# Element operations of two SBUF inputs moved from GpSimd to VectorE, squares and the convolution's first term to ScalarE, in a two-layer encoder trunk

## The chip, the core and the metric

The kernel runs on one core of one Trainium2 chip. The metric is the device time of one execution in microseconds (us), the median over runs. VectorE is called DVE here, ScalarE ACT, GpSimd POOL, the matrix engine (TensorE) PE and its weight loads PEld, SyncE SP, as in the profile. Every engine works through its own queue strictly in order, and waits at the head of the queue until what the next instruction needs is there.

## What is computed

A trunk of two layers over 1024 frames of width 1024, all in float32. The reference, cut to what matters:

```python
c_act = silu(c)
mod = c_act @ ada_w[layer] + ada_b[layer]          # six vectors of shift, scale and gate
hn = modulate(rms_norm(h, norm1_g[layer]), sh1, sc1)
# layer 0: z = hn @ w_in; gate, xr = split(z); xr = causal_depthwise_conv(xr, conv_w, conv_b)
#   r, i = sigmoid(block products of xr); a = exp(-8 r softplus(-lam)); scan a*h + mult*(i*xr)
#   y = (scan * gelu(gate)) @ w_out
# layer 1: y = chunked attention of own queries against keys and values shared from layer 0
h = h + g1 * y
hn = modulate(rms_norm(h, norm2_g[layer]), sh2, sc2)
h = h + g2 * (square(relu(hn @ w1)) @ w2)
```

The result has to agree with this in float32, so each product is made of three fast ones: every operand is split into a rounded high part and the rest, its low part, and `mm3` adds high*high, high*low and low*high.

## The kernel before

Frames lie along the free axis in two halves of 512, features along the 128 partitions. ACT makes each high part with a copy, and another engine the low part with a subtraction. Seven stretches follow each other:

- To about 100 us: norm of x, modulation, the first three products (`sq_b`, `normed`, `moded`, `lows`).
- To about 420 us, called the recurrent stretch here: for each of 11 column tiles a gate and a recurrent product, the width-4 convolution (`conv`, L700: a first term on DVE at L703, three further taps at L706), the split of its result (L283), and for each of 16 blocks of 88 features the gates and the scan (`lru`, L728: sums and products on DVE at L756 to L761, the product i*x on POOL at L759). Weight low parts are made at L192, here by POOL, since `ws.lo_engine` starts as POOL. Between these DVE makes the modulation vectors by multiplying rows of `ada` with c (L310). POOL also multiplies the scan's result by the gate (`flush`, L724) and splits it (`split_yg`, L772).
- To about 545 us: the output projection, with the residual added by DVE (L584); then to 617 us the second norm, the plain first quarter of the MLP, and the sums and splits of its operands (`NormS.mod`, `NormS.sums`, `part`).
- 617 to 917 us, the first MLP product of layer 0: 14 steps (`Quads.step`), each of seven products of 12 matmuls, in the manner of Strassen. A step needs sums of weight blocks (`add_quad`, four instructions at L124, on POOL), the splits of weights and of their sums (ACT L188, low parts L192 on DVE), the reads of the seven results (ACT L1104 for the first three, DVE L1106 for three that add, ACT L1109 for the last), relu and square (DVE L1042 and L1110), and sums of hidden blocks that are then stored to memory (`store`, four instructions at L1032, on POOL). Up to three L310 are put between.
- 917 to 1250 us, the second MLP product: 15 steps of the same form; the hidden blocks are loaded back and split (L192 on DVE, twelve of the first ones on POOL through `eng=G`), and all seven results are added by DVE (L1127).
- 1250 to 1860 us: queries, keys, values, attention and its projection.
- 1866 to 2536 us: the MLP of layer 1, with no L310 in it; its first product takes 1930 to 2207 us.

What sets the order: outside the MLPs a scheduler does. Within them the order is written out by hand: a tick passes after each of the seven products; weight sums are issued no sooner than two ticks behind the issue of their loads (`LAG`), low parts wait in the list `ws.los` and are let out by `Stream.flush`, those for DVE up to three half tiles a tick and those for POOL at once; `store` puts its jobs 1, 3 and 7 ticks later. A step's results use three PSUM banks; a bank that a second product adds to is free again once the first has been read, and two products lie between.

## Time and profile before

| | |
|---|---|
| median of 3 runs | 2536.57 us (2536.54 to 2541.02) |
| profiled execution: its own time, and the span from first to last instruction | 2537.57 us, 2535.7 us |
| granted TensorE clock, mean over the span | 0.963 |
| PE, PEld busy | 2318.8 us, 1953.4 us |
| DVE, ACT, POOL busy | 1881.2 us, 1132.7 us, 1158.5 us |
| instructions of DVE, ACT, POOL | 2300, 1835, 792 |

Busy time is the time in which an engine has an instruction in work. Matmuls are pipelined, so a busy PE is not necessarily one at its full rate; the count of matmuls in a stretch of time tells that better. A group's row gives line, engine, operation, output and inputs, shape, the count, then the busy time and the mean of one in ns, and last the engine's idle time just ahead of these instructions with what ended it. Rows of stretches give for each engine its busy time and count, then the granted clock, the share of time that the DMA engines were busy, and GB/s.

### The profile page before, as it was taken

What the parts mean: (1) busy time and instruction counts of PE and PEld (TensorE: products, weight loads), DVE (VectorE), ACT (ScalarE), POOL (GpSimd) and SP (SyncE); (2) the same over time, 40 slices, a digit from 0 to 9 for tenths busy, and PEclk for the clock granted to TensorE, in tenths of its full rate; (3) what the DMA queues carried; (4) which work ended last, traced back from release to release, by engine and by line L of the source; (5) the groups of instructions that cost most, each with busy time, mean ns of one, the idle gap of its engine ahead of it and who ended that gap; (6) DMA issues with size and microseconds to landing.
All of it is one profiled execution on the core that took longest, in us unless ns stands there. A gap on an engine that the chain in (4) does not pass through costs nothing.

```text
span 2535.7 us, 31960 instructions
## 1 busy us (share of the span) xinstructions
PE 2318.8 (91%) x11740; PEld 1953.4 (77%) x11740; DVE 1881.2 (74%) x2300; ACT 1132.7 (45%) x1835; POOL 1158.5 (46%) x792
## 2 busy tenths in 40 slices
PE   4989876987999969999999999999998999889999
PEld 3767654866777857888899998998876888667887
DVE  8879887678888877778675466998377656767776
ACT  5577653344222333334354216998153332433342
POOL 3535434337676763332011026885047666642322
PEclk9989897998999989999999999999999999999999
DMA  7323455213565576545444300012313454765444
GB/s 289 116 79 82 111 158 177 66 71 129 194 229 214 198 244 200 153 150 170 152 132 132 117 5 11 10 28 87 126 38 121 163 182 158 238 230 159 139 151 142
DMA packets 138061, 351.93 MB, mean 139 GB/s; under 512 B 14160, under 2 KB 16336, under 8 KB 137904
## 3 DMA queue, kind: packets, MB, share of 16 engines
q1 hardware_dynamic: 114080, 278.45, 34.4%
q10 hardware_dynamic: 23824, 71.44, 7.4%
q8 instruction: 92, 1.51, 0.3%
q14 instruction: 65, 0.53, 0.1%
HBM read 254.42 MB, written 83.89 MB: 133 GB/s over the span
## 4 chain that ended last, share of the span: by engine, by line
PE 56%; DVE 19%; DMA 8%; ACT 8%; issue 5%; POOL 4%; SPq 1%; ACTq 0%; DVEq 0%; POOLq 0%
PE b L278 17%; PE b L279 17%; PE b L277 17%; DMA ws<-in_ada_dram 3%; DVE s L310 2%; POOL ws L124 2%; DMA ws<-in_w_dram 2%; DVE s L192 2%; DVE ws L310 2%; PE b L1467 1%; DVE wl L192 1%; ACT s L1437 1%; DVE s L706 1%; ACT s L282 1%; ACT wh L188 1%
## 5 line engine op out<-in xcount | busy, mean ns | idle before, releaser
L277 PE MATMUL b<-s,wh 128*128 128x512 f32 x2532 | 1006.4, 401 | 115.7 <-DVE s L1106 31.3
L278 PE MATMUL b<-s,wh 128*128 128x512 f32 x2532 | 1009.3, 399 | 50.4 <-DVE s L283 42.5
L279 PE MATMUL b<-s,wl 128*128 128x512 f32 (+1 forms) x2296 | 911.4, 397 | 5.3 <-POOL wl L192 4.0
L277 PEld LDWEIGHTS b<-s,wh 128*128 128x128 f32 x2532 | 484.8, 192 | 240.1 <-DVE s L1106 34.7
L278 PEld LDWEIGHTS b<-s,wh 128*128 128x128 f32 x2532 | 486.3, 192 | 164.9 <-DVE s L283 46.2
L188 ACT ACTIVATE wh<-ws 128x1024 fp32r<-128x1024 f32 (+1 forms) x302 | 293.1, 974 | 569.3 <-POOL ws L124 298.7
L279 PEld LDWEIGHTS b<-s,wl 128*128 128x128 f32 (+1 forms) x2296 | 438.6, 191 | 104.9 <-POOL wl L192 5.3
L192 DVE TENSOR_TENSOR wl<-ws,wh 128x1024 fp32r<-128x1024 f32 (+1 forms) x212 | 322.3, 1522 | 137.4 <-ACT wh L188 120.4
L124 POOL TENSOR_TENSOR ws<-ws,ws 128x512 f32<-128x512 f32 x145 | 237.1, 1635 | 69.0 <-DMA ws<-in_w_dram 61.5
L124 POOL TENSOR_TENSOR ws<-ws 128x512 f32<-128x512 f32 x53 | 74.6, 1407 | 407.8 <-DMA ws<-in_w_dram 315.1
L192 DVE TENSOR_TENSOR s<-ws,s 128x512 fp32r<-128x512 f32 x238 | 227.7, 964 | 2.6 <-ACT s L188 2.6
L1127 DVE SCALAR_TENSOR_TENSOR s<-b,mod,s 128x512 f32<-128x512 f32 x221 | 165.0, 746 | 81.0 <-PE b L279 81.0
L277 PE MATMUL b<-wh,s 128*128 128x256 f32 x768 | 217.5, 285 | 2.6 <-ACT s L501 1.6
L279 PE MATMUL b<-wh,s 128*128 128x256 f32 x768 | 215.1, 284 | 3.5 <-DVE s L502 2.4
L278 PE MATMUL b<-wl,s 128*128 128x256 f32 x768 | 217.0, 284 | 0.0
L1032 POOL TENSOR_TENSOR s<-s,s 128x512 f32<-128x512 f32 x96 | 166.1, 1731 | 49.4 <-DMA hid<-s 44.4
L188 ACT ACTIVATE s<-ws 128x512 fp32r<-128x512 f32 x262 | 151.8, 618 | 64.1 <-PE b L279 30.8
L310 DVE CUSTOM_DVE_ANT_0 ws<-ws,cb,vec 128x1024 f32<-128x1024 f32 x64 | 96.5, 1511 | 110.5 <-DMA ws<-in_ada_dram 110.5
L192 POOL TENSOR_TENSOR wl<-ws,wh 128x1024 fp32r<-128x1024 f32 (+2 forms) x37 | 96.5, 2614 | 150.8 <-ACT wh L188 150.7
L277 PEld LDWEIGHTS b<-wh,s 128*128 128x128 f32 x768 | 147.9, 193 | 3.2 <-ACT s L501 1.8
L279 PEld LDWEIGHTS b<-wh,s 128*128 128x128 f32 x768 | 146.6, 193 | 4.3 <-DVE s L502 3.0
L278 PEld LDWEIGHTS b<-wl,s 128*128 128x128 f32 x768 | 148.0, 193 | 0.3 <-issue 0.2
(182 smaller groups left out, 3396.4 us busy)
## 6 DMA issues: line engine op xcount, KB each, us to landing
hid<-s ACTq DMA_DIRECT2D x128, 512.0 KB
ws<-hid SPq DMA_DIRECT2D x118, 512.0 KB
ws<-in_w_dram SPq DMA_DIRECT2D x220, 256.0 KB
ws<-in_ada_dram SPq DMA_DIRECT2D x64, 512.0 KB
s<-in_ada_dram SPq DMA_DIRECT2D x32, 512.0 KB
ws<-in_w_in_dram SPq DMA_DIRECT2D x22, 512.0 KB
hsp<-s SPq DMA_DIRECT2D x32, 256.0 KB
s<-in_kvada_dram SPq DMA_DIRECT2D x16, 512.0 KB
```

The costliest lines, as they stand in the source:

```text
L124: G.tensor_tensor(out=out, in0=in0, in1=in1, op=op)
L188: self.nc.scalar.activation(out=hi[:rows, :n], in_=src, func=AF.Copy)
L192: (it["eng"] or self.lo_engine).tensor_tensor(out=lo[:rows, :n], in0=src, in1=hi[:rows, :n].bitcast(F32), op=ALU.subtract)
L277: PE.matmul(ps, ah, bh, start=start, stop=False, skip_group_check=more)
L278: PE.matmul(ps, ah, bl, start=False, stop=False, skip_group_check=more)
L279: return PE.matmul(ps, al, bh, start=False, stop=stop, skip_group_check=more).ins
L282: A_.activation(out=hi, in_=src, func=AF.Copy)
L310: V.tensor_tensor_reduce(out=t, in0=t, in1=cb, op0=ALU.mult, op1=ALU.add, scale=1.0, scalar=bias, accum_out=dst)
L706: V.scalar_tensor_tensor(out=y[:, d:], in0=xr[:, : S - d], scalar=vc("cw", (3 - d) * NT + t), in1=y[:, d:], op0=ALU.mult, op1=ALU.add)
L1032: G.tensor_tensor(out=out, in0=in0, in1=in1, op=ALU.subtract)
L1127: V.scalar_tensor_tensor(out=t, in0=ps, scalar=g2[:, m : m + 1], in1=t, op0=ALU.mult, op1=ALU.add)
L1437: A_.activation(out=p[:, lo:640], in_=p[:, lo:640], func=AF.Exp, scale=-1.0, bias=m, accum_out=s1)
```

## The change

420 instructions leave POOL. Its remaining work is the weight sums of the second MLP products from the third step on, and what attention gives it. DVE takes over all the others: 61 low parts of weights and hidden blocks (L192), 128 sums of hidden blocks (L1032), 128 of the 236 weight-sum instructions (L124), the low parts of norms and of the gated result (L499, L537, L772, L818), sums of the norms (L552, L801), and the products L724 and L759. DVE gives away the convolution's first term (L703), which ACT makes while it reads the result from PSUM, and all squares behind relu (L1042, L1055, L1110): `relu2` is now two ACT instructions, relu and square, and for the three results that DVE adds they are issued one tick later. ACT's `Identity` with a bias and a DVE instruction replace two ACT copies where POOL had made the low part (`modulate`). `Stream.flush` lets out four half tiles a tick, not three, and `store` puts its jobs 2, 4 and 8 ticks later. The diff, cut to its core:

```diff
-    def add_quad(self, a11, a12, a21, a22, n):
+    def add_quad(self, a11, a12, a21, a22, n, eng):
...
-                G.tensor_tensor(out=out, in0=in0, in1=in1, op=op)
+                eng.tensor_tensor(out=out, in0=in0, in1=in1, op=op)
...
             def low():
-                (it["eng"] or self.lo_engine).tensor_tensor(
+                self.nc.vector.tensor_tensor(
                     out=lo[:rows, :n], in0=src, in1=hi[:rows, :n].bitcast(F32), op=ALU.subtract)
...
-    def flush(self, most=3):
+    def flush(self, most=4):
...
-            ws.add_quad(u[:, :512], u[:, 512:], v[:, :512], v[:, 512:], 512)
+            ws.add_quad(u[:, :512], u[:, 512:], v[:, :512], v[:, 512:], 512, V)
...
-            ws.add_quad(*(I["w2"][l][s % 4][x][:, c] for x in range(4)), 512)
+            ws.add_quad(*(I["w2"][l][s % 4][x][:, c] for x in range(4)), 512, G if s > 1 else V)
...
-        if pool:
-            A_.activation(out=t, in_=t, func=AF.Identity, bias=sh[:, k : k + 1])
-            N.lastact = A_.activation(out=hi, in_=t, func=AF.Copy).ins
-            G.tensor_tensor(out=lo, in0=t, in1=hi.bitcast(F32), op=ALU.subtract)
-        else:
-            A_.activation(out=hi, in_=t, func=AF.Identity, bias=sh[:, k : k + 1])
-            V.scalar_tensor_tensor(out=lo, in0=t, scalar=sh[:, k : k + 1], in1=hi.bitcast(F32),
-                                   op0=ALU.add, op1=ALU.subtract)
+        A_.activation(out=hi, in_=t, func=AF.Identity, bias=sh[:, k : k + 1])
+        V.scalar_tensor_tensor(out=lo, in0=t, scalar=sh[:, k : k + 1], in1=hi.bitcast(F32),
+                               op0=ALU.add, op1=ALU.subtract)
...
         A_.activation(out=xraw[t][:, hs(half)], in_=ps, func=AF.Copy)
+        A_.activation(out=xc[t][:, hs(half)], in_=ps, func=AF.Identity,
+                      scale=vc("cw", 3 * NT + t), bias=vc("cb", t))
...
-        V.tensor_scalar(out=y, in0=xr, scalar1=vc("cw", 3 * NT + t), scalar2=vc("cb", t),
-                        op0=ALU.mult, op1=ALU.add)
...
-            G.tensor_tensor(out=yg[u], in0=yg[u], in1=ym[u], op=ALU.mult)
+            V.tensor_tensor(out=yg[u], in0=yg[u], in1=ym[u], op=ALU.mult)
...
-            G.tensor_tensor(out=i_, in0=i_, in1=x, op=ALU.mult)
+            V.tensor_tensor(out=i_, in0=i_, in1=x, op=ALU.mult)
...
-        G.tensor_tensor(out=b, in0=yg[k], in1=a.bitcast(F32), op=ALU.subtract)
+        split(yg[k], a, b)
...
-                    G.tensor_tensor(out=out, in0=in0, in1=in1, op=ALU.subtract)
+                    V.tensor_tensor(out=out, in0=in0, in1=in1, op=ALU.subtract)
...
-            for d, job in ((1, squares), (3, sums), (7, rest_)):
+            for d, job in ((2, squares), (4, sums), (8, rest_)):
...
-        def relu2(t):
-            V.scalar_tensor_tensor(out=t, in0=t, scalar=0.0, in1=t, op0=ALU.max, op1=ALU.mult)
+        def relu2(t, src=None):
+            A_.activation(out=t, in_=t if src is None else src, func=AF.Relu)
+            A_.activation(out=t, in_=t, func=AF.Square)
...
                     V.tensor_tensor(out=t, in0=t, in1=ps, op=ALU.add)
-                    relu2(t)
+                    jobs.append((now[0] + 1, lambda: relu2(t)))
```

How DVE's queue changes, at two places (the names are tiles: s work tiles, ws loaded weights or `ada` rows, wh and wl high and low parts of weights, b PSUM banks; numbers tell buffers apart). The first is the recurrent stretch, around one tile's convolution. Before, DVE has here the split of a block (L283), two `ada` rows (L310, each with a short read of its sum), the first term (L703) and the three taps (L706):

```order
L283 TENSOR_TENSOR s_1910<-s_1776,s_1909 88x1024
L310 ISA ws_2182,mod_82<-ws_2182,cb,vec 128x1024
L310 ISA mod_82 128x1
L703 TENSOR_SCALAR s_1972<-s_1938,vec 128x1024
L706 SCALAR_TENSOR_TENSOR s_1972<-s_1938,vec,s_1972 128x1023
L706 SCALAR_TENSOR_TENSOR s_1972<-s_1938,vec,s_1972 128x1022
L706 SCALAR_TENSOR_TENSOR s_1972<-s_1938,vec,s_1972 128x1021
```

After, with the lines of the changed kernel (L280 is the split, L307 an `ada` row, L692 a tap, L710 the product with the gate, L190 a weight's low part):

```order
L710 TENSOR_TENSOR s_1289<-s_1289,s_1649 128x1024
L280 TENSOR_TENSOR s_1918<-s_1784,s_1917 88x1024
L190 TENSOR_TENSOR wl_1978<-ws_1397,wh_1977 88x704
L692 SCALAR_TENSOR_TENSOR s_1947<-s_1946,vec,s_1947 128x1023
L307 ISA ws_2192,mod_82<-ws_2192,cb,vec 128x1024
L307 ISA mod_82 128x1
L692 SCALAR_TENSOR_TENSOR s_1947<-s_1946,vec,s_1947 128x1022
L692 SCALAR_TENSOR_TENSOR s_1947<-s_1946,vec,s_1947 128x1021
```

The first term is gone from DVE, and two instructions that POOL had, L710 and L190, stand ahead of the taps.

The second place is one step of layer 0's first MLP product, near its end. Before (L1106 adds a result, L1042 and L1110 are relu and square, L192 low parts of weights):

```order
L1106 TENSOR_TENSOR s_5384<-s_5384,b_5387 128x512
L1042 SCALAR_TENSOR_TENSOR s_5384<-s_5384 128x512
L192 TENSOR_TENSOR wl_5474<-ws_5238,wh_5473 128x1024
L1106 TENSOR_TENSOR s_5384<-s_5384,b_5388 128x512
L1042 SCALAR_TENSOR_TENSOR s_5384<-s_5384 128x512
L1106 TENSOR_TENSOR s_5385<-s_5385,b_5386 128x512
L1042 SCALAR_TENSOR_TENSOR s_5385<-s_5385 128x512
L192 TENSOR_TENSOR wl_5512<-ws_5241,wh_5511 128x1024
L192 TENSOR_TENSOR wh_5516<-ws_5279,wh_5516 128x512
L192 TENSOR_TENSOR wl_5554<-ws_5339,wh_5553 128x1024
```

After (L122 are the weight sums, L1079 adds a result, L1005 are the hidden sums, L190 the low parts):

```order
L122 TENSOR_TENSOR ws_5381<-ws_5464 128x512
L122 TENSOR_TENSOR ws_5426<-ws_5464,ws_5381 128x512
L122 TENSOR_TENSOR ws_5423<-ws_5426,ws_5464 128x512
L122 TENSOR_TENSOR ws_5423<-ws_5426,ws_5423 128x512
L1079 TENSOR_TENSOR s_5428<-s_5428,b_5431 128x512
L190 TENSOR_TENSOR wl_5519<-ws_5279,wh_5518 128x1024
L1079 TENSOR_TENSOR s_5428<-s_5428,b_5432 128x512
L1079 TENSOR_TENSOR s_5429<-s_5429,b_5430 128x512
L1005 TENSOR_TENSOR s_5285<-s_5284,s_5285 128x512
L1005 TENSOR_TENSOR s_5284<-s_5284 128x512
L1005 TENSOR_TENSOR s_5284<-s_5284,s_5285 128x512
L1005 TENSOR_TENSOR s_5285<-s_5285,s_5284 128x512
```

The weight sums now stand in DVE's queue ahead of the three additions, and the hidden sums of the step before behind them; relu and square are gone from it.

More of the change, by code (lines that the diff above doesn't have):

```diff
@@ L198, in step @@
             if self.timed:
-                self.los.append((it["eng"] or self.lo_engine, n / HALF, low))
+                self.los.append((n / HALF, low))
             else:
@@ L208, in step @@
                 self.live["u"] -= 1
-    def flush(self, most=3):
+    def flush(self, most=4):
         late = []
         for low in self.los:
-            if low[0] is self.nc.vector:
-                if most <= 0:
-                    late.append(low)
-                    continue
-                most -= low[1]
-            low[2]()
+            if most <= 0:
+                late.append(low)
+                continue
+            most -= low[0]
+            low[1]()
         self.los = late
@@ L386, in hid_item @@
             src = hid[p : p + 2, :, HID.index(nm)].rearrange("a p b -> p a b")
-        it = ws.item([(0, n * HALF, src)], [(x * HALF, HALF, True) for x in range(n)], to="a",
-                     eng=G if v == 2 and n == 2 and what[1][0] == 3 and nm != "B11" else None)
+        it = ws.item([(0, n * HALF, src)], [(x * HALF, HALF, True) for x in range(n)], to="a")
         for x, w in enumerate(what):
@@ L526, in mod, with part @@
                 A_.activation(out=t, in_=t, func=AF.Identity, bias=self.sh[:, k : k + 1])
-                self.part(t, f"B{1 + k // 4}{1 + half}", k % 4, G if k % 2 else V)
-        def part(self, src, name, k, eng):
+                self.part(t, f"B{1 + k // 4}{1 + half}", k % 4)
+        def part(self, src, name, k):
             o = slot(F32R)
@@ L536, in low @@
             def low():
-                eng.tensor_tensor(out=lo, in0=src, in1=hi.bitcast(F32), op=ALU.subtract)
+                V.tensor_tensor(out=lo, in0=src, in1=hi.bitcast(F32), op=ALU.subtract)
                 self.op[name, k] = (hi, lo)
             if ws.timed:
-                ws.los.append((eng, 1, low))
+                ws.los.append((1, low))
             else:
@@ L814, in moded, with lows @@
             A_.activation(out=hi, in_=t, func=AF.Copy)
-        def lows(k, half, E):
+        def lows(k, half):
             t, hi, lo = (a[k][:, hs(half)] for a in (xt, n1.hh, n1.hl))
-            E.tensor_tensor(out=lo, in0=t, in1=hi.bitcast(F32), op=ALU.subtract)
+            V.tensor_tensor(out=lo, in0=t, in1=hi.bitcast(F32), op=ALU.subtract)
         V.tensor_tensor(out=cb, in0=cb, in1=sgm, op=ALU.mult)
```

83 lines of the change are left out of this document (30 added, 53 removed).

## The prediction

> **What bounds the kernel now.** I read the span, then the busy time by stretches, then PE's waits. The kernel's own time was 2537.57 us in the profiled execution, 1.0 us above the median of 2536.57, and the span of its instructions is this:
>
> ```profile
> span 2535.7 us, 31960 instructions
> ```
>
> The stretches are the recurrent part, the projection with the norm and the MLP's plain quarter, layer 0's first and second MLP products, layer 1's plain quarter with its first product, its second product, and last, for the rate, 50 us in the middle of a second product. Columns: busy us (instructions) of PE, PEld, DVE, ACT, POOL, then granted clock, DMA share, GB/s.
>
> ```profile
> 100.00:420.00 320.00, 262.66 (x1076) 205.01 (x1075) 260.76 (x185) 200.16 (x226) 132.86 (x47) 0.89 0.40 119
> 420.00:617.00 197.00, 172.55 (x712) 136.97 (x711) 146.98 (x156) 83.17 (x116) 89.73 (x45) 0.92 0.26 86
> 617.00:917.00 300.00, 275.46 (x1165) 224.31 (x1166) 250.73 (x225) 93.40 (x130) 210.57 (x118) 0.96 0.62 216
> 917.00:1200.00 283.00, 269.04 (x1153) 219.26 (x1154) 215.01 (x255) 108.69 (x165) 106.87 (x68) 0.98 0.55 176
> 1866.00:2207.00 341.00, 318.66 (x1383) 261.50 (x1384) 229.75 (x217) 125.25 (x181) 218.83 (x142) 0.97 0.44 153
> 2207.00:2536.00 329.00, 311.01 (x1332) 252.80 (x1330) 239.27 (x286) 115.98 (x175) 113.02 (x71) 0.98 0.52 168
> 1100.00:1150.00 50.00, 50.00 (x222) 41.40 (x221) 40.55 (x52) 21.10 (x32) 13.91 (x9) 1.00 0.55 166
> ```
>
> In the last row PE never pauses and does 222 matmuls in 50 us: 0.2252 us each. At that rate a stretch's count gives its floor: 1076 matmuls 242.3 us in the recurrent stretch, so 77.7 of its 320 us are lost; 712 give 160.3, lost 36.7; 1165 give 262.4, lost 37.6; 1153 give 259.7, lost 23.3; 1383 give 311.5, lost 29.5; 1332 give 300.0, lost 29.0. The lost time holds PE's pauses and the lowered clock behind them (0.89 in the recurrent stretch). Most of it is in the two stretches in which DVE is over 80% busy, and PE waits for DVE first (total us, times, longest):
>
> ```profile
> PE b L278 <- DVE s L283: 42.5, 7, 12.7
> PE b L277 <- DVE s L1106: 31.3, 8, 9.3
> ```
>
> L283 belongs to the recurrent stretch, L1106 to the first MLP products. So the question is what DVE's queue becomes.
>
> **What POOL costs DVE.** First two DVE groups from 1200 to 1250 us, where POOL rests, then the same DVE instruction and POOL's from 903 to 930 us, where both work:
>
> ```profile
> L192 DVE TENSOR_TENSOR wl<-ws,wh 128x1024 fp32r<-128x1024 f32 x6 | 7.3, 1219 | 0.0
> L192 DVE TENSOR_TENSOR s<-ws,s 128x512 fp32r<-128x512 f32 x10 | 6.5, 690 | 0.0
> ```
>
> ```profile
> L192 DVE TENSOR_TENSOR s<-ws,s 128x512 fp32r<-128x512 f32 x10 | 15.6, 1586 | 0.0
> ```
>
> ```profile
> L192 POOL TENSOR_TENSOR s<-ws,s 128x512 fp32r<-128x512 f32 x10 | 17.2, 1742 | 1.6 <-ACT s L188 1.6
> ```
>
> A half tile takes DVE 690 ns alone and 1586 beside POOL; POOL needs 1742. So one half tile on each engine holds both for some 1.7 us, and two in a row on DVE alone take 1.38. Work moved to DVE is thus paid for by what DVE no longer loses.
>
> **Part by part: the recurrent stretch.** DVE's and POOL's groups from 100 to 420 us, and an `ada` row's price with POOL at rest (1390 to 1450 us):
>
> ```profile
> L310 DVE CUSTOM_DVE_ANT_0 ws<-ws,cb,vec 128x1024 f32<-128x1024 f32 x29 | 48.7, 1682 | 35.4 <-DMA ws<-in_ada_dram 35.4
> L761 DVE TENSOR_TENSOR_SCAN s<-s,s 88x1024 f32<-88x1024 f32 x14 | 31.8, 2280 | 0.2
> L706 DVE SCALAR_TENSOR_TENSOR s<-s,vec,s 128x1023 f32<-128x1023 f32 x10 | 30.7, 3072 | 0.3
> L706 DVE SCALAR_TENSOR_TENSOR s<-s,vec,s 128x1022 f32<-128x1022 f32 x10 | 25.0, 2501 | 0.3
> L703 DVE TENSOR_SCALAR s<-s,vec 128x1024 f32<-128x1024 f32 x10 | 20.9, 2088 | 3.1 <-ACT s L698 3.1
> L283 DVE TENSOR_TENSOR s<-s,s 88x1024 fp32r<-88x1024 f32 x14 | 20.8, 1510 | 6.8 <-ACT s L282 6.8
> L760 DVE TENSOR_TENSOR s<-s,s 88x1024 f32<-88x1024 f32 x14 | 19.2, 1370 | 0.0
> L756 DVE SCALAR_TENSOR_TENSOR s<-s,s 88x1024 f32<-88x1024 f32 x14 | 19.2, 1375 | 12.6 <-ACT s L754 12.6
> L757 DVE SCALAR_TENSOR_TENSOR s<-s,s 88x1024 f32<-88x1024 f32 x14 | 19.1, 1365 | 0.2
> L706 DVE SCALAR_TENSOR_TENSOR s<-s,vec,s 128x1021 f32<-128x1021 f32 x10 | 18.2, 1816 | 0.3
> ```
>
> ```profile
> L759 POOL TENSOR_TENSOR s<-s,s 88x1024 f32<-88x1024 f32 x14 | 43.7, 3127 | 6.3 <-ACT s L743 6.3
> L192 POOL TENSOR_TENSOR wl<-ws,wh 128x1024 fp32r<-128x1024 f32 x16 | 42.3, 2646 | 75.4 <-ACT wh L188 75.4
> L724 POOL TENSOR_TENSOR s<-s,s 128x1024 f32<-128x1024 f32 x8 | 23.4, 2928 | 86.4 <-DMA s<-s 86.4
> ```
>
> ```profile
> L310 DVE CUSTOM_DVE_ANT_0 ws<-ws,cb,vec 128x1024 f32<-128x1024 f32 x11 | 14.1, 1285 | 37.9 <-DMA ws<-in_ada_dram 37.9
> ```
>
> What DVE loses: L310 29 x (1.682 - 1.285) = 11.5; the taps L706, at L310's price since no row shows them alone, 10 x (3.072 + 2.501 + 1.816 - 3 x 1.285) = 35.3; L703 leaves with 20.9; L283 14 x (1.510 - 1.219) = 4.1; L760, L756 and L757 14 x (1.370 + 1.375 + 1.365 - 3 x 1.219) = 6.3. Together 78.1 us. What it gains, at 1.219: L759 17.1, L192 19.5, L724 9.8, and nine more POOL instructions that these rows leave out, at most 11.0: 57.4. Net 20.7 less, so DVE goes from 260.8 to about 240 us, still beside 59 us in which it waits, over half of it for `ada` rows (35.4). Those waits I leave as they are. Each L759 is now ready 1.9 us sooner; of 14 x 1.9 = 27 I count half on the path, 13. So 34 us, with 0 and 63 as ends: nothing, if transfers and scans (2.28 each, never slowed) set the pace; 63, if only 15 of the 77.7 lost stay. ACT's 20 or so extra first terms cost at least 0.6 each (a PSUM read, below) and I allow twice that, 24: ACT is then 224 of some 286 us busy, which hides them.
>
> **Layer 0's first MLP product,** 617 to 917 us, DVE, POOL and one ACT group:
>
> ```profile
> L192 DVE TENSOR_TENSOR wl<-ws,wh 128x1024 fp32r<-128x1024 f32 x41 | 77.9, 1899 | 19.9 <-ACT wh L188 13.2 <-POOL s L1032 6.7
> L310 DVE CUSTOM_DVE_ANT_0 s<-s,cb,vec 128x1024 f32<-128x1024 f32 x30 | 59.0, 2004 | 2.6 <-DMA s<-in_ada_dram 2.5
> L1042 DVE SCALAR_TENSOR_TENSOR s<-s 128x512 f32<-128x512 f32 x42 | 41.0, 976 | 1.4
> L1106 DVE TENSOR_TENSOR s<-s,b 128x512 f32<-128x512 f32 x42 | 28.6, 681 | 25.1 <-PE b L279 16.4 <-issue 4.1 <-ACT wh L188 3.5
> L192 DVE TENSOR_TENSOR wh<-ws,wh 128x512 fp32r<-128x512 f32 x14 | 23.7, 1694 | 0.0
> ```
>
> ```profile
> L1032 POOL TENSOR_TENSOR s<-s,s 128x512 f32<-128x512 f32 x45 | 81.9, 1822 | 24.3 <-DMA hid<-s 21.9
> L124 POOL TENSOR_TENSOR ws<-ws,ws 128x512 f32<-128x512 f32 x40 | 75.5, 1888 | 2.1
> L1032 POOL TENSOR_TENSOR s<-s 128x512 f32<-128x512 f32 x15 | 26.6, 1770 | 1.2
> L124 POOL TENSOR_TENSOR ws<-ws 128x512 f32<-128x512 f32 x13 | 20.0, 1539 | 60.8 <-DMA ws<-in_w_dram 38.0 <-DVE s L1042 11.8 <-DMA hid<-s 10.3
> ```
>
> ```profile
> L1104 ACT ACTIVATE s<-b 128x512 f32<-128x512 f32 x42 | 25.0, 598 | 99.4 <-PE b L279 77.1 <-POOL s L1032 14.4 <-DVE s L1055 7.8
> ```
>
> L1106, with one input in PSUM, takes 681 ns even here: only instructions with two SBUF inputs suffer. DVE loses 41 x (1.899 - 1.219) = 27.9, 30 x (2.004 - 1.285) = 21.6, 14 x (1.694 - 0.690) = 14.1, and L1042's 41.0: 104.6. It gains 45 + 40 + 15 + 13 = 113 half tiles at 0.690: 78.0. Net 26.6 less: 250.7 becomes 224, below PE's floor of 262. PE sets the pace then, and the chain behind a weight sum is shorter: four of POOL's at 1.8 in a row took 7.2 us, ACT and DVE's low parts waited for them, and L1106 stood behind those; on DVE they take 2.8. I count 26 of the 37.6 lost; 11 stay for the filling at the start. Ends: 0, and 34. ACT gains relu and square for L1042, 84 x 0.598 = 50 us on 93.4: hidden while it stays below PE's pace; uncovered it would cost those 50.
>
> One rule speaks against this edit. The Trainium skill (ScalarE: Activation LUTs, Rules for kernel authors) says that relu and multiplication belong on VectorE, not ScalarE. By it, L1042's 42 would stay on DVE at 0.690, and DVE would have 253 us, still under the floor of 262: the sum would be the same.
>
> **The rest.** The other four rows lost 36.7, 23.3, 29.5 and 29.0 us. They hold the same mixture at smaller size, but the second products keep their POOL sums, and much of their loss is their start, where transfers run. I take a third of each: 39.5, and for the ends nothing and a half (59). Attention, queries and the first 100 us I leave at zero: their DVE load changes little either way.
>
> Sum: 34 + 26 + 39 = 99 us; 2537.6 - 99 = 2438.6, and 1.0 less against the median: **2437 us**.
>
> **Rivals.**
>
> - Only the MLP gains. The recurrent chain stays at its `ada` waits and scans (34 not gained), and both second products keep their starts (8 + 9): 48 gained, 2489. For it: 35.4 us of DVE's waits there are for transfers.
> - Nearly all is won: 63 + 34 + 59 = 156, 2381. For it: DVE's load falls below PE's floor in both stretches.
> - Slower: the queue in order. DVE now stands at the weight sums until their transfer has landed, with the three additions and the low parts behind it, and PE behind those. POOL waited 60.8 us ahead of 14 such sums, 4.3 each. With 32 quads of sums on DVE, each passing its 4.3 us on to PE, 139 us go: 2537 - 99 + 139 = 2577. It decides if the wait is longer than the two products (24 x 0.2252 = 5.4 us) that a bank's reading may take. Against it: those 60.8 us are partly waits for DVE itself.
> - No change. The two engines share something, and work moved between them takes the same from both: 2537. The Trainium skill (Perfetto Trace Analysis, Optimizing Scalar/DVE Operations) says that VectorE and GpSimd share an SBUF read port, so that moving operations between the two might not help. The rows bear out the sharing, 1586 against 690, but POOL's own 1742 for a half tile is what goes.
> - It doesn't do what it says: DVE is slowed by something else than POOL, and the new half tiles take 1.586 too. Then the first product gets 113 x 1.586 - 41 = 138 us more on DVE, 389 in place of 300: 2626. Against it: L1106's 681.
>
> **Chances.** Forecast 0.56, MLP only 0.18, nearly all 0.12, no change 0.04, queue in order 0.08, not POOL 0.02. The range goes from 2375 to 2500, so that it holds the first three cases. Its own range for the forecast is 2400 to 2475. A measurement of this kernel tells about 0.2% from no change. Faster 0.86, same 0.04, slower 0.10.
>
> **What would show it.** Right: L706's taps at about 1.3 us, weights' low parts at 1.22 in both stretches, POOL near idle from 100 to 900 us, the recurrent stretch at some 286 us and the first product at some 274, PE's waits for L283 and L1106 halved. Wrong: a new wait of DVE for weight transfers of over 60 us in a first product with PE waiting behind it, two-input instructions that stay over 1.5 us with POOL idle, or an ACT that PE waits for.

## The result, and the profile after the change

The changed kernel takes 2475.57 us (median of 4 runs, 2473.27 to 2484.14) against 2538.80 of the kernel before (4 runs, 2536.54 to 2541.59): ratio 0.9757, 95% interval 0.973 to 0.9783. 2437 us was forecast, so 99 us less; 63 came. The time lies in the stated range of 2375 to 2500, just outside the forecast's own 2400 to 2475, and nearer the rival "only the MLP gains" (2489) than the forecast. POOL has 367 instructions in place of 792, so 425 left it. The profiled execution (2476.07 us) has this span:

```profile
span 2474.3 us, 31665 instructions
```

To see where they came from, I cut both traces at the same pieces of work; "first" and "last" mean the start of such an instruction. The last row ends with the end of the last instruction of PE, DVE, ACT or POOL.

| part, up to | before, us | after, us | won | forecast |
|---|---|---|---|---|
| first addition of the output projection (L584; L572 after): the recurrent part | 417.0 | 399.9 | 17.1 | 34 |
| first read of layer 0's first product (L1104; L1077) | 200.0 | 184.1 | 15.9 | 12 |
| first addition of its second product (L1127; L1099) | 304.6 | 296.6 | 8.0 | 26 |
| last addition of it | 329.7 | 330.5 | -0.8 | 8 |
| first read of layer 1's first product (L1104; L1077), attention among it | 678.0 | 667.6 | 10.4 | these two: 10 |
| first addition of its second product | 281.9 | 271.1 | 10.8 | |
| the end | 321.7 | 321.5 | 0.2 | 9 to 10 |

The stretches as in the prediction, in the changed kernel (busy us and instructions of PE, PEld, DVE, ACT, POOL, granted clock, DMA share, GB/s):

```profile
100.00:403.00 303.00, 258.42 (x1044) 200.20 (x1043) 227.11 (x219) 205.89 (x237) 0.00 (x0) 0.89 0.40 118
403.00:584.00 181.00, 170.10 (x731) 136.41 (x729) 138.16 (x186) 92.42 (x130) 0.00 (x0) 0.98 0.27 89
584.00:880.00 296.00, 277.28 (x1176) 222.68 (x1176) 209.24 (x296) 147.98 (x231) 0.00 (x0) 0.98 0.65 225
880.00:1163.00 283.00, 267.24 (x1152) 217.97 (x1153) 212.98 (x269) 108.54 (x166) 81.67 (x52) 0.98 0.55 175
1816.00:2146.00 330.00, 325.10 (x1434) 267.89 (x1433) 221.45 (x307) 191.10 (x299) 0.00 (x0) 1.00 0.46 159
2146.00:2474.00 328.00, 307.62 (x1329) 250.93 (x1327) 238.22 (x302) 118.41 (x179) 87.69 (x56) 0.98 0.53 170
```

At 0.2252 us a matmul these lose 67.9, 16.4, 31.2, 23.6, 7.1 and 28.7 us, after 77.7, 36.7, 37.6, 23.3, 29.5 and 29.0. Layer 1's first product stands within some 7 us of PE's floor now, the second products are where they were, and layer 0's first product still loses 31. In it these are groups of DVE (line, operation, shapes, count, then busy us, mean ns, idle us before them and what ended it):

```profile
L190 DVE TENSOR_TENSOR wl<-ws,wh 128x1024 fp32r<-128x1024 f32 x42 | 51.4, 1223 | 31.9 <-ACT wh L186 31.8
L307 DVE CUSTOM_DVE_ANT_0 s<-s,cb,vec 128x1024 f32<-128x1024 f32 x32 | 39.5, 1280 | 0.0
L1005 DVE TENSOR_TENSOR s<-s,s 128x512 f32<-128x512 f32 x45 | 31.1, 690 | 1.0
...
L122 DVE TENSOR_TENSOR ws<-ws,ws 128x512 f32<-128x512 f32 x40 | 27.6, 690 | 0.9
...
L122 DVE TENSOR_TENSOR ws<-ws 128x512 f32<-128x512 f32 x13 | 9.0, 692 | 46.4 <-DMA ws<-in_w_dram 46.4
```

The prices hold: 690 ns for half a tile, 1223 for a low part, 1280 for an `ada` row. But DVE stands 46.4 us at the first of each four weight sums (L122), and 31.8 at low parts whose high part ACT hasn't made. PE's waits in the whole kernel begin with these; L280 and L1079 are the L283 and L1106 of before:

```profile
PE b L275 <- DVE s L280: 41.3, 9, 9.1
...
PE b L274 <- DVE s L1079: 15.9, 11, 3.8
```

In the recurrent stretch (85 to 398 us) the same picture, DVE's groups and then its waits:

```profile
L307 DVE CUSTOM_DVE_ANT_0 ws<-ws,cb,vec 128x1024 f32<-128x1024 f32 x30 | 38.2, 1279 | 25.6 <-DMA ws<-in_ada_dram 25.6
...
L745 DVE TENSOR_TENSOR s<-s,s 88x1024 f32<-88x1024 f32 x14 | 17.0, 1217 | 4.1 <-ACT s L729 4.0
...
L692 DVE SCALAR_TENSOR_TENSOR s<-s,vec,s 128x1023 f32<-128x1023 f32 x11 | 14.0, 1276 | 0.1
```

```profile
DVE ws L307 <- DMA ws<-in_ada_dram: 25.6, 14, 5.2
DVE s L742 <- ACT s L740: 25.4, 9, 4.6
DVE s L280 <- ACT s L279: 7.3, 2, 3.9
DVE s L710 <- DMA s<-s: 7.1, 4, 3.6
```

The taps take 1.276 us in place of up to 3.07. DVE is busy 233.4 us from 85 to 398, against 270.0 from 85 to 415 before: 36.6 less. But its waits rose from 59.7 to 78.5 us: those for rows fell from 37.2 to 25.6, those at L742 for ACT rose from 12.6 to 30.2. Work and waits together fill the stretch in either trace, so 36.6 less work with 18.8 more waiting is the 17 won, told another way, and not yet a cause.

### The profile page after: what moved, and what is told of

Same layout as the page of the kernel before. It is cut to its first block, busy times and chain, and to the rows that moved or that the text cites. A ratio compares the mean times of both kernels' runs of the same rounds, so it can differ in the third digit from the quotient of the medians.

```text
span 2474.3 us, 31665 instructions
## 1 busy us (share of the span) xinstructions
PE 2308.5 (93%) x11740; PEld 1945.8 (79%) x11740; DVE 1761.3 (71%) x2586; ACT 1257.6 (51%) x2054; POOL 370.7 (15%) x367
## 4 chain that ended last, share of the span: by engine, by line
PE 52%; DVE 16%; ACT 14%; DMA 10%; issue 6%; POOL 1%; SPq 0%; ACTq 0%; DVEq 0%; POOLq 0%
PE b L275 16%; PE b L276 16%; PE b L274 16%; DMA ws<-in_w_dram 3%; DMA ws<-in_ada_dram 2%; ACT wh L186 2%; DVE wl L190 2%; DVE s L307 2%; PE b L1437 1%; ACT s L1407 1%; DMA s<-hsp 1%; POOL ws L122 1%; ACT s L279 1%; DMA hid<-s 1%; DVE s L1079 1%
## 5 line engine op out<-in xcount | busy, mean ns | idle before, releaser
L274 PE MATMUL b<-s,wh 128*128 128x512 f32 x2532 | 1000.8, 399 | 74.1 <-ACT wh L186 17.8
L275 PE MATMUL b<-s,wh 128*128 128x512 f32 x2532 | 1003.8, 397 | 45.0 <-DVE s L280 41.3
L190 DVE TENSOR_TENSOR wl<-ws,wh 128x1024 fp32r<-128x1024 f32 (+1 forms) x249 | 305.6, 1229 | 162.7 <-ACT wh L186 160.3
L122 POOL TENSOR_TENSOR ws<-ws 128x512 f32<-128x512 f32 x21 | 27.9, 1327 | 1618.4 <-DMA ws<-in_w_dram 1579.2
L1099 DVE SCALAR_TENSOR_TENSOR s<-b,mod,s 128x512 f32<-128x512 f32 x221 | 165.0, 747 | 81.9 <-PE b L276 81.3
L190 DVE TENSOR_TENSOR s<-ws,s 128x512 fp32r<-128x512 f32 x262 | 210.8, 820 | 1.4 <-ACT s L186 1.4
L1015 ACT ACTIVATE s<-s 128x512 f32<-128x512 f32 x84 | 53.0, 631 | 201.7 <-DVE s L1079 181.4
L307 DVE CUSTOM_DVE_ANT_0 ws<-ws,cb,vec 128x1024 f32<-128x1024 f32 x64 | 81.7, 1281 | 99.9 <-DMA ws<-in_ada_dram 99.9
L1206 ACT ACTIVATE s<-b 128x256 f32<-128x256 f32 x96 | 31.2, 381 | 127.2 <-PE b L276 114.3
L276 PE MATMUL b<-s,wh 128*128 128x512 f32 x236 | 93.9, 398 | 0.0
```

The source lines that it names most:

```text
L122: eng.tensor_tensor(out=out, in0=in0, in1=in1, op=op)
L190: self.nc.vector.tensor_tensor(out=lo[:rows, :n], in0=src, in1=hi[:rows, :n].bitcast(F32), op=ALU.subtract)
L274: PE.matmul(ps, ah, bh, start=start, stop=False, skip_group_check=more)
L275: PE.matmul(ps, ah, bl, start=False, stop=False, skip_group_check=more)
L276: return PE.matmul(ps, al, bh, start=False, stop=stop, skip_group_check=more).ins
L307: V.tensor_tensor_reduce(out=t, in0=t, in1=cb, op0=ALU.mult, op1=ALU.add, scale=1.0, scalar=bias, accum_out=dst)
```

## The experiments

First idea: the transfers of the `ada` rows hold layer 0's first product, since layer 1's has no rows and runs at PE's floor. Rivals: DVE's own time for the rows; or DVE standing at the weight sums in the order of its queue. Each time is the median of 4 to 12 executions, with 9 to 17 of the kernel before beside them (2537.66 to 2539.17 us; 4 beside the changed kernel). The parts below, in us, are cut as above: recurrent part; layer 0's first and second product; layer 1's first and second. They are from one trace each; that of three ticks is of its fastest execution, 2447.26 us.

| kernel | time | ratio to before (95%) | rec. | 0, first | 0, second | 1, first | 1, second |
|---|---|---|---|---|---|---|---|
| changed kernel | 2475.57 | 0.9757 (0.973-0.9783) | 399.9 | 296.6 | 330.5 | 271.1 | 321.5 |
| rows not transferred | 2467.42 | 0.9719 (0.9705-0.9734) | 396.3 | 289.0 | 332.1 | 273.8 | 321.8 |
| rows transferred, not multiplied | 2453.11 | 0.9655 (0.9638-0.9672) | 397.4 | 276.1 | 330.4 | 272.8 | 321.4 |
| weight sums on POOL | 2471.14 | 0.9733 (0.9718-0.9748) | 397.8 | 286.8 | 331.3 | 273.3 | 321.2 |
| before, rows not transferred | 2541.03 | 1.0004 (0.999-1.0018) | 417.1 | 302.3 | 328.4 | 282.5 | 322.2 |
| weight sums after three ticks | 2453.42 | 0.9654 (0.9633-0.9674) | 396.8 | 280.7 | 325.8 | 272.7 | 316.1 |
| three ticks, sums on POOL | 2462.20 | 0.9686 (0.9664-0.9709) | 398.9 | 284.5 | 327.5 | 273.9 | 317.1 |
| three ticks, rows moved | 2470.26 | 0.9718 (0.97-0.9736) | 398.1 | 276.1 | 344.5 | 273.1 | 318.3 |
| relu on DVE | 2490.66 | 0.9807 (0.9788-0.9825) | 396.7 | 305.4 | 332.3 | 278.1 | 320.6 |
| recurrent rows not transferred | 2458.28 | 0.9677 (0.9661-0.9692) | 386.5 | 296.6 | 330.6 | 273.2 | 321.3 |
| fewer table loads | 2462.28 | 0.9693 (0.9671-0.9715) | 390.1 | 294.8 | 329.0 | 271.5 | 321.6 |
| first term on DVE | 2474.32 | 0.9737 (0.9721-0.9753) | 395.6 | 292.5 | 331.5 | 273.1 | 322.5 |
| i*x on POOL | 2471.14 | 0.9727 (0.9706-0.9748) | 393.6 | 297.8 | 330.3 | 271.6 | 322.4 |

Where a part is untouched, it says how far one trace can be trusted: layer 0's first product lies between 292.5 and 297.8 in the five kernels that leave the MLP as the change has it, the recurrent part between 396.3 and 399.9 in eight.

**Rows not transferred, in the changed kernel and in the one before.**

```diff
-                ws.item([(0, 1024, src)], [], to="u", raw=False, use=use)
+                ws.item([], [], to="u", raw=False, use=lambda t, use=use: use(t, cb))
```

> The changed kernel, with the transfers of the 32 `ada` rows in layer 0's first MLP product left out: VectorE makes the same 32 products, but of a tile that is already there, so the modulation vectors are not the reference's. In the changed kernel this product took 294 us (584 to 878 us) and layer 1's, which has no rows, 268. Theory: the transfers of the rows hold this product, as they make the weights land late. Then it takes about 270 us and the whole about 2452 (24 less than 2476). First rival: VectorE's own time for the rows (39.5 us) holds it, then nothing changes: 2476. Second rival: VectorE stands at the weight sums in any case, since it takes them in order; then its waits for weights stay near the 46.4 us of now, and at most 5 us go.

> The kernel before, with the transfers of the 32 `ada` rows in layer 0's first MLP product left out as in the run on the changed kernel; VectorE makes the same products of a tile that is there. That product took 300 us (617 to 917 us) and layer 1's 277. By the theory that the rows' transfers held this product already before the change, it falls to about 278, and the whole from 2538 to about 2516. By the step of the prediction, that what VectorE loses beside GpSimd (104.6 us) held it, it stays at 295 to 300, and the whole at 2533 to 2538.

In the changed kernel the product went to 289.0, which is 8 us less and not the 24 of the first idea; the second rival had allowed 5. DVE's waits at the sums shrank little: 38.6 us are left of 46.4. Before the change, 302.3 for 304.6: nothing clear of the spread. My first idea fell; transfers are at most 8 of the 25 us by which layer 0's product is longer than layer 1's.

**Rows transferred, not multiplied.** DVE takes one element of each partition; it still waits for the landing.

```diff
+            if small:
+                V.tensor_tensor(out=dst, in0=t[:, 0:1], in1=bias, op=ALU.add)
```

> The changed kernel, with the 32 `ada` rows of layer 0's first MLP product still transferred, but VectorE takes one element of each partition in place of the product with c (about 0.17 us for 1.28, 36 us less in sum), so the modulation vectors are not the reference's. By the theory of the transfers the product still takes 288 to 294 us, the whole 2470 to 2476. By the rival that VectorE's time for the rows holds it, it falls to about 270, the whole to about 2452.

276.1 and 2453.11 us, near the rival's 270 and 2452. And DVE stands even longer at the sums here, by its waits from 583 to 857 us; the second row is its wait for ACT's high parts:

```profile
DVE ws L122 <- DMA ws<-in_w_dram: 51.4, 13, 6.9
DVE wl L190 <- ACT wh L186: 36.1, 21, 2.7
```

So standing alone does no harm: PE's waits for the additions fall from 14.6 to 3.5 us here. It harms an engine with too much work beside it: in the changed kernel 207.2 us of work (584 to 878 us), 46.4 of standing and 31.8 of waits for ACT fill 285 of 294 us. That sum proves nothing by itself, since waits take whatever time the work leaves: with rows not multiplied the same three fill 259 of 274 us. What differs is the work, 171.8 us for 207.2.

**Weight sums on POOL.**

```diff
-            ws.add_quad(u[:, :512], u[:, 512:], v[:, :512], v[:, 512:], 512, V)
+            ws.add_quad(u[:, :512], u[:, 512:], v[:, :512], v[:, 512:], 512, G)
```

> The changed kernel with the weight sums of both first MLP products on GpSimd again, as before the change; all else as changed. By the rival that VectorE loses by standing at the weight sums (46.4 us in 12 waits in layer 0's product, with the additions behind them and TensorE's 14.6 us of waits for L1079 behind those), layer 0's product falls from 294 to about 280 and the whole to about 2462. By the theory of the transfers the weights are late for either engine, and layer 0's product stays at 290 to 300; beside 53 half tiles a layer on GpSimd, VectorE's instructions with two inputs in SBUF become longer again, and the whole is 2476 to 2490.

286.8: undoing this part of the change wins 10 us there, of the 14 that the queue was to win. The whole kernel's gain, 4 us in place of 14, is within its uncertainty. POOL now does the standing, and DVE's instructions beside it are longer again (584 to 868 us; POOL's waits, then two groups of DVE):

```profile
POOL ws L122 <- DMA ws<-in_w_dram: 135.3, 10, 24.9
```

```profile
L190 DVE TENSOR_TENSOR wl<-ws,wh 128x1024 fp32r<-128x1024 f32 x41 | 56.4, 1375 | 37.0 <-ACT wh L186 36.9
L307 DVE CUSTOM_DVE_ANT_0 s<-s,cb,vec 128x1024 f32<-128x1024 f32 x32 | 50.8, 1625 | 1.8 <-DMA s<-in_kvada_dram 1.7
```

That is 41 x (1.375 - 1.223) + 32 x (1.625 - 1.280) = 17 us of loss beside POOL, and it is less than what the standing costs. In layer 1, where DVE has 170 us of work in 268, the same edit shows nothing (273.3 for 271.1).

**Weight sums after three ticks,** still on DVE; and as a control the same with the sums on POOL.

```diff
-    LAG = {"p": 2, "w": 0, "a": 2, "u": 4}
+    LAG = {"p": 3, "w": 0, "a": 2, "u": 4}
```

> The changed kernel with the weight sums (and only they) issued no sooner than three ticks behind their loads, in place of two, in all MLP products; they stay on VectorE in the first products. Theory, formed after four runs: VectorE's queue holds layer 0's first product, since it works 207 us there, stands 46.4 us at weight sums whose loads have not landed, and TensorE waits for the additions behind them; sums on GpSimd took that product from 296.6 to 286.8 us, rows that VectorE hardly reads took it to 276.1. If it is the standing, a tick more (2.7 us) takes about 12 x 2.7 = 32 us of the 46.4 away, the product falls to about 287 and the whole to about 2466. Rival: the load of VectorE alone decides, and GpSimd's run gained by the 37 us of sums that it took; then nothing changes (2476), or it loses as the weights' splits come a tick later (2480 to 2490).

> The changed kernel with both edits that helped: weight sums three ticks behind their loads, and those of the first products on GpSimd. A control for the run with three ticks alone (layer 0's first product 280.7 us, the whole 2453). By the theory that three ticks help since VectorE no longer stands at the sums, they bring nothing in a first product where GpSimd stands in its place: it stays at 284 to 290 us (286.8 with two ticks), and only the second products win their 4 to 5 us each: 2459 to 2468. By the rival that a later place in the order helps by itself, it falls to 281 or below, the whole to 2455 or less.

280.7 and 2453.42 us, better than the 287 and 2466 expected: this one number in the source beats both kernels clearly. From 580 to 861 us DVE now waits first for PE, which is as it should be where PE sets the pace, and little of the standing is left:

```profile
DVE s L1079 <- PE b L276: 33.8, 13, 3.5
DVE ws L122 <- DMA ws<-in_w_dram: 8.9, 8, 2.6
DVE wl L190 <- ACT wh L186: 8.3, 8, 2.3
```

DVE's work is as before, 211.8 us in this stretch, so the rival that its load alone decides is out. The control shows that it was DVE's standing and not the later place as such: with the sums on POOL a tick more wins 2.3 us (286.8 to 284.5), on DVE 15.9. With the standing DVE's waits for ACT fell too, from 31.8 to 8.3, and the runs don't separate the two. The second products win 4 to 5 us in both. Whether three ticks would have helped the kernel before was not tried.

**Three ticks, rows moved.** 17 of the 32 rows leave the first product, and layer 0's second product issues two a step from its third step on. That makes 24 in twelve steps: seven more rows than those 17, drawn forward from later parts of the kernel.

```diff
-            ada_late(0 if l or q in (2, 15) else 2 if q in (3, 8, 13, 14) else 3)
+            ada_late(0 if l or q in (2, 15) else 2 if q % 4 == 3 else 1)
...
+                if l == 0 and s > 1:
+                    ada_late(2)
```

> The changed kernel with weight sums three ticks behind their loads, and with 17 of the 32 `ada` rows of layer 0's first MLP product moved into its second product. By the load of VectorE, 17 x 1.28 = 22 us leave the first product; since its queue no longer stands and TensorE waits there for 5 us only, I expect 280.7 to become 275 to 279, and the second product to stay at 326 to 328, the whole 2447 to 2452. Rival: the second product, where VectorE also works about 240 of 326 us and each addition is read by VectorE, pays as much: 2453 to 2458.

The first product fell as expected (276.1), and the second grew from 325.8 to 344.5, more than the rival had, and the whole to 2470.26. DVE has 30 us more work there, which is the 24 rows at their usual price, as the two kernels' second products show, with three ticks alone and with the rows moved (then the rows' group):

```profile
861.00:1187.00 326.00, 312.78 (x1365) 256.79 (x1366) 242.11 (x319) 129.12 (x195) 81.79 (x52) 0.98 0.55 180
```

```profile
860.00:1204.00 344.00, 319.56 (x1360) 253.65 (x1361) 272.38 (x367) 130.00 (x195) 85.35 (x52) 0.98 0.60 207
```

```profile
L307 DVE CUSTOM_DVE_ANT_0 s<-s,cb,vec 128x1024 f32<-128x1024 f32 x24 | 30.4, 1282 | 2.7 <-DMA s<-in_ada_dram 1.7 <-DMA s<-in_kvada_dram 0.8
```

So 17 rows alone were not tried; 24 cost the second product 19 us.

**Relu and square on DVE.**

```diff
-            A_.activation(out=t, in_=t if src is None else src, func=AF.Relu)
-            A_.activation(out=t, in_=t, func=AF.Square)
+            if src is not None:
+                A_.activation(out=t, in_=src, func=AF.Relu)
+                V.tensor_tensor(out=t, in0=t, in1=t, op=ALU.mult)
+            else:
+                V.scalar_tensor_tensor(out=t, in0=t, scalar=0.0, in1=t, op0=ALU.max, op1=ALU.mult)
```

> The changed kernel with relu and square of the first products on VectorE again (one instruction of some 0.69 us for each result that VectorE adds, one square for the others; some 39 us more VectorE in each first product, some 45 us less ACT). By the prediction, which saw VectorE below TensorE's floor there, nothing changes: 2476. By the theory that VectorE's queue is full in layer 0's first product (207 us of work, 46 of standing at sums, 32 of waits for ACT in 294), it grows by 15 to 25 us, layer 1's by 0 to 5, the whole to 2490 to 2505.

15 us slower, 9 in layer 0's first product and 7 in layer 1's. The whole is what the theory of the full queue had, 2490 to 2505, but by two parts that both missed: 15 to 25 and 0 to 5 were expected. From 584 to 880 us, the stretch, then DVE's standing, then PE's wait behind it:

```profile
584.00:880.00 296.00, 270.05 (x1162) 219.18 (x1160) 236.96 (x342) 90.52 (x126) 0.00 (x0) 0.98 0.61 216
```

```profile
DVE ws L122 <- DMA ws<-in_w_dram: 47.9, 13, 4.9
```

```profile
PE b L274 <- DVE s L1082: 16.9, 9, 3.1
```

237 of work and 48 of standing leave DVE 11 of 296 us, and PE does 1162 matmuls where the changed kernel did 1176. The prediction had held 253 us of DVE to be free. The Trainium skill (ScalarE: Activation LUTs, Rules for kernel authors) puts relu and multiplication on VectorE; this run differs, by 15 us. For the single result the price does favour DVE, with one instruction of 690 ns for two of 631 and 633 on ACT. Another of its pages (Perfetto Trace Analysis, Optimizing Scalar/DVE Operations) says that with VectorE saturated, giving work to ScalarE may make sense; with that the run agrees in layer 0. Layer 1's product loses 7 us though DVE has only 212 us of work in 278 there. Those 7 us I can place only in part: PE's listed waits there rise from 3.7 to 6.8 us, the most of it for ACT's reads.

**The recurrent stretch: rows not transferred, and fewer table loads.** The first takes the transfers of 30 rows away (the scheduler then issues some other transfers in another order), the second puts a copy in place of the square root. Not all of ACT's 28 table loads around it go: nine stay ahead of the exponential (L740). In the changed kernel (85 to 398 us), then in this one (85 to 386 us):

```profile
L738 ACT ACT_TABLE_LOAD x14 | 18.0, 1283 | 0.3
L740 ACT ACT_TABLE_LOAD x14 | 18.0, 1283 | 0.1
```

```profile
L740 ACT ACT_TABLE_LOAD x9 | 11.5, 1283 | 0.1
```

So 19 loads go, 24 us of ACT's work and not 36.

```diff
-                ws.add(*rest.pop(0))
+                _s, _n, use = rest.pop(0)
+                ws.item([], [], to="u", after=ws.items[-1], use=lambda t, use=use: use(t, cb))
```

```diff
-            A_.activation(out=v, in_=tau, func=AF.Sqrt)
+            A_.activation(out=v, in_=tau, func=AF.Copy)
```

> The changed kernel with the transfers of the 30 or so `ada` rows in the recurrent stretch left out: VectorE makes the same products of a tile that is already there, so the modulation vectors are not the reference's. Up to the first addition of the output projection the changed kernel takes 400 us, the kernel before 417. Theory: a loop through the queues of ACT and VectorE sets the pace (VectorE waits 25.4 us for ACT's L740 and TensorE 40 us for VectorE's L280), so that VectorE's 25.6 us of waits for rows turn into waits for ACT: 393 to 400, the whole 2469 to 2476. Rival: the rows' transfers, 15 % of the chain that ended last in this stretch, set the pace: about 380, the whole about 2456.

> The changed kernel with a copy in place of the square root in the recurrent unit, so that ACT needs no table loads around it (28 of 1.283 us, 36 us in sum, of ACT's 211 us of work in 313 us); the result is not the reference's. By the theory that the loop through ACT sets the pace, the recurrent part falls from 400 to about 375 (VectorE's 25.4 us of waits for L740 go) and the whole to about 2451. By the rival that the rows' transfers, or VectorE's own work, set it: at most 5 us, 2471 or more.

386.5 and 390.1: 10 to 13 us and 6 to 10 us less than the eight kernels' 396.3 to 399.9, and in neither run does a theory have the part's number. (Without the transfers the whole, 2458.28, is close to the rival's 2456, but 7 us of that come later, between layer 0's second product and layer 1's first.) Without the rows' transfers DVE waits longer for ACT (the line is L740 of the changed kernel), without the table loads it still waits for the rows (85 to 381 and 85 to 386 us):

```profile
DVE s L743 <- ACT s L741: 37.8, 12, 5.7
```

```profile
DVE ws L307 <- DMA ws<-in_ada_dram: 24.2, 13, 5.2
DVE s L742 <- ACT s L740: 14.6, 5, 3.4
```

Taking the rows' 25.6 us of waits away wins about half of that, taking 24 us of ACT's work away a quarter to two fifths; the rest comes back at the next wait.

**The convolution's first term on DVE, and the product i*x on POOL.**

```diff
-        A_.activation(out=xc[t][:, hs(half)], in_=ps, func=AF.Identity,
-                      scale=vc("cw", 3 * NT + t), bias=vc("cb", t))
...
+        V.tensor_scalar(out=y, in0=xr, scalar1=vc("cw", 3 * NT + t), scalar2=vc("cb", t),
+                        op0=ALU.mult, op1=ALU.add)
```

```diff
-            V.tensor_tensor(out=i_, in0=i_, in1=x, op=ALU.mult)
+            G.tensor_tensor(out=i_, in0=i_, in1=x, op=ALU.mult)
```

> The changed kernel with the convolution's first term on VectorE again, as before the change: ACT loses 22 reads of 0.773 us (17 us), VectorE gains 11 instructions of some 0.7 to 1.3 us (8 to 14 us) in the recurrent stretch. If ACT is what the loop waits for, the recurrent part stays at 400 or falls by up to 8 us; if VectorE's own work sets the pace, it grows by 8 to 14, the whole to 2484 to 2490.

> The changed kernel with one kind of instruction given back to GpSimd: the recurrent unit's product i*x (14 to 16 of them, 3.127 us each on GpSimd before the change, 1.217 on VectorE after). By the prediction's prices VectorE's other instructions with two inputs in SBUF become longer beside 44 us of GpSimd work, and each product comes 1.9 us later, so that the part up to the first addition of the output projection grows from 400 to 405 to 415, the whole to 2481 to 2491. Rival: what this stretch gained came from elsewhere (the order, the convolution's first term), and it stays within 3 us: 2473 to 2479.

Both make no difference that can be measured in the whole (2474.32 and 2471.14), and the part is 1 to 6 us shorter than in the eight kernels (395.6 and 393.6 us), not longer. The first falls within what was expected if ACT is waited for; 8.8 us more of DVE's work (11 first terms of 804 ns) cost nothing, so the growth of 8 to 14 us is out. The 5 to 15 us of the second expectation were wrong. With i*x on POOL, 14 products (17 us) leave DVE, and its busy time hardly moves (85 to 395 us):

```profile
85.00:395.00 310.00, 266.03 (x1080) 207.00 (x1080) 231.28 (x218) 209.02 (x242) 38.03 (x14) 0.90 0.43 126
```

In the changed kernel the same 310 us had 230.44 of DVE:

```profile
85.00:395.00 310.00, 265.42 (x1075) 205.98 (x1075) 230.44 (x228) 210.67 (x244) 0.00 (x0) 0.89 0.42 125
```

What DVE saves it loses to instructions that run beside POOL, here `ada` rows and the last taps, by its groups:

```profile
L307 DVE CUSTOM_DVE_ANT_0 ws<-ws,cb,vec 128x1024 f32<-128x1024 f32 x30 | 44.2, 1479 | 25.5 <-DMA ws<-in_ada_dram 25.5
...
L692 DVE SCALAR_TENSOR_TENSOR s<-s,vec,s 128x1021 f32<-128x1021 f32 x11 | 18.1, 1647 | 0.2
```

This is the exchange that the prediction had as its rival "no change", true for this one instruction. The Trainium skill (Perfetto Trace Analysis, Optimizing Scalar/DVE Operations) says that moving work between the two might not help, as they share a read port; the two rows of stretches agree with it here. The weight sums agree only in part: 37 us of them on POOL left DVE 193.07 us of work (584 to 868 us) in place of 207.2.

## Why the prediction was right, and where it was not

**The sign and the prices were right.** With POOL at rest DVE's instructions took what the rows of quiet stretches had shown (690, 1223, 1280 ns; taps 1276), and two terms came out larger than forecast: 15.9 for 12 ahead of layer 0's first product, and 21.2 for 10 from layer 0's second product to layer 1's, where layer 1's first product went to PE's floor. DVE even lost more work than counted: 227.1 us in the recurrent stretch (100 to 403) for the 240 forecast, 207.2 in layer 0's first product for 224. The prediction had left out the squares at L1110, 12.1 us in that product, and what L758 lost. Only 63 of the 99 us came, because two terms were mis-sized and the terms of the second products (8 and 9 to 10) came to nothing; those keep their sums on POOL, and their starts. That the sum was off by 36 us and no more is partly luck: the two terms that came out larger cover 15 of the 53 that the others missed. And the two stretches with a busy DVE did not hold most of PE's lost time, as the prediction says, but half, 115 of 234 us.

**The step that failed most: "below PE's floor of 262. PE sets the pace then"** (26 us, measured 8). It compared DVE's work with PE's floor and left out that DVE's queue can stand. I had noted that POOL waited 60.8 us ahead of its weight sums, and had moved that wait with the instructions in a rival only, not in this term. It moved: 46.4 us of standing and 31.8 of waits for ACT beside 207 us of work, and 0.6 us in which DVE waited for PE. The runs with sums on POOL (10 us back) and with a tick more before the sums (16 us back) show it, the control with both shows that it is DVE's standing, and the run with rows hardly read shows that the standing costs only beside enough work. With the sums on DVE, layer 0's product goes roughly with work and standing taken together, here over the whole product and against a floor of 265 us (1176 matmuls of 0.2252):

| kernel | work + standing, us | product, us |
|---|---|---|
| three ticks, rows moved | 190 + 0 | 276.1 |
| three ticks | 212 + 9 | 280.7 |
| rows transferred, not multiplied | 174 + 51 | 276.1 |
| rows not transferred | 210 + 39 | 289.0 |
| changed kernel | 210 + 46 | 296.6 |
| relu on DVE | 246 + 48 | 305.4 |

The sum need not reach the floor: at 256 of 265 us the product is already 16 to 20 us longer than at 225 or less.

So the rival "the queue in order" was real as a term of some 16 us, not as an outcome of 139. Its threshold, waits longer than 5.4 us, was wrong too: of the 12 waits, 3.9 us on average, one is longer (5.8). In layer 1, without rows, 20.7 us of standing cost nothing that shows.

**"The sum would be the same" with relu on VectorE** was wrong by the same step: 9 us in this product, 15 in the whole. ACT's two instructions were not wholly hidden either: relu stands in ACT's queue until DVE has added, ahead of high parts, and DVE waits 31.8 us for those, 2.1 in the run with relu on DVE. The 39 us that they take off DVE are worth more.

**"Only instructions with two SBUF inputs suffer"** was wrong too. L758 and the first term read one tile each, and they were slowed as well: the first term took 2088 ns beside POOL's work. L758 before (100 to 420 us), the same instruction after (85 to 398 us), and the first term back on DVE with POOL at rest (85 to 395 us):

```profile
L758 DVE TENSOR_SCALAR s<-s 88x1024 f32<-88x1024 f32 x14 | 13.8, 990 | 0.0
```

```profile
L744 DVE TENSOR_SCALAR s<-s 88x1024 f32<-88x1024 f32 x13 | 8.7, 675 | 0.0
```

```profile
L690 DVE TENSOR_SCALAR s<-s,vec 128x1024 f32<-128x1024 f32 x11 | 8.8, 804 | 0.0
```

**The recurrent term (34, measured 17).** It had two pieces. Half of the earlier i*x, 13 us, was wrong: with i*x back on POOL, where it takes 2.72 us for DVE's 1.22, the time does not grow. The other took DVE's shorter work as won, and of the waits beside it said: "Those waits I leave as they are." They did not stay so:

```profile
85.00:415.00 330.00, 275.50 (x1137) 215.65 (x1135) 270.03 (x208) 199.18 (x226) 137.35 (x49) 0.90 0.40 119
```

```profile
85.00:398.00 313.00, 268.42 (x1088) 208.47 (x1088) 233.41 (x232) 210.84 (x245) 0.00 (x0) 0.89 0.42 125
```

DVE's 36.6 us less work came with 18.8 us more waiting. PE's waits for L280, forecast to halve, stayed (41.3 for 42.5). No single cause was found that sets the pace there: the rows' transfers and 19 table loads give 10 to 13 and 6 to 10 us when taken away, 8.8 us more of DVE's work cost nothing, and nothing gives all. So what the 17 us came from stays open. How much of them is POOL's absence and how much the new order was not separated; low parts and the products with the gate were not put back on POOL alone.

**Of the signs named in advance,** the taps, the low parts, an idle POOL and the halved wait for L1106 (15.9 for 31.3) came; the recurrent stretch at 286 and the first product at 274 us did not, and the wait of DVE for weights, put at over 60 us as a sign of failure, was 46.4 and did its harm below that.

## What to carry to other kernels

When an instruction moves to another engine, move its wait with it: add the new standing to the engine's work, and compare that sum with the floor, not the work alone. With the 60.8 us that stood in the rows of before, it would have been 224 + 61 = 285 against 262. A sum a little under the floor is no safety either; here 256 of 265 still cost 16 to 20 us. If the sum comes near, first try to issue the waiting instruction later; one number, a tick more ahead of the weight sums, won 22 us here, about a third of what the whole change had. In the recurrent stretch, where engines wait in turn for each other, work or waits that were taken off one engine were won by half or less, as the next wait grew.

## What the runs showed of the hardware

DVE's instructions between SBUF tiles were slowed only while POOL worked at that moment. In the trace of before, from 85 to 917 us, 11 low parts (L192, 128x1024) ran with no POOL instruction beside them and took 1.22 us on average; the 41 others took 2.05. Of the one-input L758, 13 ran alone at 0.67 us and 3 beside POOL at 2.88. L1106, with one input in PSUM, took 0.69 alone and 0.68 beside. Of the 16 scans all but one ran alone, so the traces don't tell whether POOL slows those. With i*x alone on POOL, `ada` rows went from 1.279 to 1.479 us, the last tap from 1.276 to 1.647, and the split L280, which then never met POOL, stayed at 1.213. A switch of ACT's function table took 1.283 us, twice around each square root.
